# A two-layer hybrid block on one core: normed activations in one tile per chunk, and a pad ahead of the gated tiles

## The chip, the cores and the metric

The kernel runs on one core of one Trainium2 chip. The metric is device time in microseconds (us); the median of three runs of the kernel before is 1625.59 us (1624.21 to 1625.91).

## The reference

Two layers (DEPTH = 2) work on 256 latent tokens and 256 context tokens of width 1024, in float32. Each layer is a half-step SwiGLU FFN, a mixing stage of four head groups (Fourier, latent attention, spatial gating, pooling) between one input and one output projection, and a second half-step FFN. Norms are modulated by vectors computed from a conditioning vector with a 1024 x 9216 matrix per layer.

```python
def ffn_half_step(h, g, shift, scale, gate, w13, w2):
    return h + 0.5 * gate * swiglu(modulate(rms_norm(h, g), shift, scale), w13, w2)
...
def swiglu(x, w13, w2):
    a, b = jnp.split(x @ w13, 2, axis=-1)
    return (jax.nn.silu(a) * b) @ w2
```

with D_FF = 2816. In the last layer the context tokens are not carried past the keys and values, so the last FFN works on the 256 latent tokens alone.

## The kernel before, in words

**Layout.** Activations are feature-major: 8 chunks (KC) of 128 features on the partitions, tokens along the columns, T = 256 latent columns ("half" v = 0) and 256 context columns (v = 1). The residual stream h stays in SBUF. Weights come from HBM as half-units of 128 x 1024 float32 (512 KB), each loaded by the SP queue into one of five staging tiles (`stg`).

**Two parts per number.** Every large product is made of three float32r matmuls (`mm3`, lines 191 to 193). ScalarE copies a staged half-unit rounded to float32r into `whi` (line 157), VectorE, or now and then GpSimd, subtracts to get the remainder `wlo` (line 165). In the same way an activation x becomes `xhi` + `xlo`. Line 191 multiplies whi by xhi, line 192 whi by xlo, line 193 wlo by xhi; all three add into one PSUM tile. The weights are the stationary operand (a 128 x 128 block of a half-unit, loaded anew for every matmul), the activations the moving one (512 columns for both halves of the tokens, 256 for one).

**The tiles of the activations.** The norm's output, and in the mixing stage the four groups' outputs, stand in `nhi0..7` and `nlo0..7`, one pair per chunk, each [128, 2T + 2] (lines 516 and 517). `n_of(c, v)` gives the slices of half v, or both halves. The gated products silu(a) b stand in `ghi0..7` and `glo0..7`, [128, 512] each, allocated in each FFN's own pool. Of the FFN's 22 k-blocks, three parts of 8, 7 and 7 are worked off in turn: the part's first products (w13 against n, "n" below), then its second products (w2 against g, "g" below). In the third part the last four output tiles are done half by half, 256 columns at a time (`final_half`).

**The last FFN's raw form.** Before the last FFN the norm's factors are not waited for: its first products take A h, with the shift as extra columns (`raw_of`, `raw_shifts`, `raw_in`), so these matmuls have 258 columns; the factor 1/rms, kept in a tile `rsb`, is multiplied in behind them. There `raw_of(c)` uses the v = 1 half and the two extra columns of nhi and nlo.

**Addresses.** SBUF tiles are placed pool after pool in the order in which the program opens them, each rounded up to 32 bytes. Per partition, in bytes: the `whi` tiles start at 76480 and the `wlo` tiles at 96960, five of 4096 bytes each; a block of weights begins at a multiple of 512 from there. So every block of weights lies at 192 modulo 256, which is called the weights' residue here. `nhi0` starts at 117440 and the sixteen nhi and nlo tiles follow with a stride of 2080 (2056 rounded up), so that their residues modulo 256 are 192, 224, 0, 32, 64, 96, 128, 160 for chunks 0 to 7, the same for nhi and nlo (nlo0 starts 16640 = 65 x 256 bytes behind nhi0). The pool `tmp` follows, and after it, from 165248 on, the pools of a stage. In the first FFN a pool `early` of 9280 bytes and a table of 8192 come before the gated tiles: they start at 182720 with strides of 2048, residue 192. In the second, third and last FFN the pool starts at 165248 and all its tiles have residue 128.

**Order of work.** The order of all instructions on each engine is fixed when the program is built. `Weaver` keeps an estimate of TensorE's time (`W.pe`) and resumes the side tasks (norms, evacuations, weight conversion, the modulation's dot products on VectorE) when their estimated turn has come; the estimated costs depend on the operands' shapes, not on their addresses.

Of the kernel before, what the change touches and what calls it, by code (L numbers as in the profile page):

```python
# [11 lines left out]
F32 = mybir.dt.float32  # L12
# [19 lines left out]

# columns of the per-layer parameter packs
PK1 = {}
# [19 lines left out]
class Weaver:  # L54
    """Keeps an estimate of TensorE's time and resumes side tasks when their turn comes."""

# [48 lines left out]
class Slots:  # L105
    """A fixed set of equal tiles, handed out in the order in which they came back."""

# [21 lines left out]
def block_kernel(ctx: ExitStack, tc: tile.TileContext, ins, out: bass.AP):  # L129
# [10 lines left out]

    # ---------------------------------------------------------------- pools
    cst = ctx.enter_context(tc.tile_pool(name="cst", bufs=1))
# [11 lines left out]

    # ---------------------------------------------------------------- engine helpers
    def act(o, i, func, after=0.0, n=None, **kw):
# [42 lines left out]

    # ---------------------------------------------------------------- the weight stream  # L200
    loads = []
# [121 lines left out]

    # ---------------------------------------------------------------- constants and residual
    ident = cst.tile([P, P], F32, name="ident")
# [40 lines left out]

    # ---------------------------------------------------------------- modulation
    mods, gains, gates, n_ada, n_mod = {}, {}, {}, {}, {}
# [14 lines left out]
    def gain_from(l, i, c0=0, c1=KC, n=2):  # L383
        """A = sqrt(D) g (1 + scale) for norm i."""
        m = mods[l][:, :n, (1, 4, 7)[i] * 8 + c0:(1, 4, 7)[i] * 8 + c1]
        vstt(gains[l][:, i, :n, c0:c1], m, 1.0,
             gains[l, "g"][:, i, None, c0:c1].to_broadcast([P, n, c1 - c0]), ALU.add, ALU.mult)
# [16 lines left out]
    def ada_quarter(q, tiles):  # L404
        """Layer 0's m0 and m1, column chunks 2q and 2q+1."""
        ps = yield from SM.get()
        for k, (when, w) in enumerate(tiles):
            yield when
            for g in range(4):
                nc.tensor.matmul(ps[32 * g:32 * g + 32, :P], sc[:, k], w[:, 128 * g:128 * g + 128],  # L410
                                 start=k == 0, stop=k == KC - 1)
            W.pe(270.0)
        yield W.t + 150.0
        sb = yield from DG.get()
        yield vcopy(sb[:, :P], ps[:, :P])
        tp = ps[:, P:]
        yield transpose(tp[:, :P], sb[:, :P])
        DG.put(sb)
        b = k1(0, "b_ada")
        for v in range(2):  # L420
            for m in range(2):
                o = 8 * m + 2 * q
                src = tp[:, :P].rearrange("p (g r) -> p g r", r=32)[:, 2 * m:2 * m + 2, v]
                vtt(mods[0][:, v, o:o + 2], src, b[:, o:o + 2], ALU.add)
        SM.put(ps)
        gain_from(0, 0, 2 * q, 2 * q + 2)
        n_ada[0] += 4
        yield W.free["v"]

    def ada_tile(j, l, i):  # L430
        """128 columns of the modulation: VectorE's dot products of w_ada's columns with silu(c)."""
        r, c = i // KC, i % KC
# [20 lines left out]

    # ---------------------------------------------------------------- norms
    last = [False]
    acc, acc_i, acc_n, acc_t, last_sq = {}, {}, {}, {}, {}

    def square_in(v, c):
        """Adds the squares of h's chunk c, half v, to half v's sum."""
        if v not in acc:  # L460
# [19 lines left out]
    def sum_of(v):  # L480
        """Waits for half v's sum of squares; gives it with the time it is there."""
        while acc_n.get(v, 0) < KC:
# [5 lines left out]
    def rstd_chain(srcs, nblk, n_feat):  # L488
        """1/sqrt(sum + n eps) of the columns of src [128, 128 nblk], broadcast over partitions (in PSUM)."""
        ps = yield from SM.get()  # L490
# [24 lines left out]
    n_time = {}  # L515
    nhi = [npl.tile([P, 2 * T + 2], F32R, name="nhi%d" % c) for c in range(KC)]
    nlo = [npl.tile([P, 2 * T + 2], F32R, name="nlo%d" % c) for c in range(KC)]

    def n_of(c, v):
        s = slice(0, 2 * T) if v is None else slice(v * T, v * T + T)  # L520
        return nhi[c][:, s], nlo[c][:, s]

    # The last norm's factors are applied behind the first products: these take A h with the shift as one more column.
    raw_done = set()
    raw_R = []

    def raw_of(c):
        return nhi[c][:, T:], nlo[c][:, T:]

    def raw_shifts(l, i):  # L530
        for c in range(KC):
            s = shift_of(l, i, 0, c).to_broadcast([P, 2])
            hi, lo = (t[:, 2 * T:] for t in (nhi[c], nlo[c]))
            yield act(hi, s, AF.Copy)
            yield vtt(lo, s, hi.bitcast(F32), ALU.subtract)

    def raw_in(l, i, c):
        hi, lo = n_of(c, 1)
        x, a = h[:, c, 0], gain_of(l, i, 0, c)
# [3 lines left out]

    def apply(l, i, v, R, c0=0, c1=KC):
        """The modulated norm of h's chunks c0..c1, half v, as an exact sum of two float32r parts."""
        prev = None
# [16 lines left out]
    def norm_task(l, i, v):  # L563
# [4 lines left out]
        if raw_done:  # L568
            R = tmp.tile([P, T], F32, name="rsb", tag="rsb", bufs=1)
            yield act(R, ps[:, :T], AF.Copy)  # L570
# [4 lines left out]

    # ---------------------------------------------------------------- GEMM pieces
    hi_ = [0]
# [9 lines left out]
    def cols(ps, vs):  # L587
        """The columns of a PSUM tile that hold the halves vs."""
        return ps[:, vs[0] * T:(vs[-1] + 1) * T]

    def gemm(i, vs, nk=KC, xs=None, ps=None, ok=None, raw=False):
        """A feature-major tile: half-unit i against all k, halves vs."""
        ps = ps or ps_new()
# [10 lines left out]
    def gemm_start(i0, vss, evacs, ks=range(KC), ok=None, raw=False):  # L604
        """The four half-units at i0, half by half, k outermost, behind what makes their operand."""
        ok = ok or (lambda v, k: n_done.get(v, 0) > k)
# [22 lines left out]

    # ---------------------------------------------------------------- FFN  # L630
    def ffn(l, which, vs, tail):
        """h += 0.5 m (silu(a) b) w2 with a, b from the norm's output. Ends with the squares of the new h."""
        i_norm = (0, 2)[which - 1]
        full = len(vs) == 2
        with tc.tile_pool(name="ffn%d%d" % (l, which), bufs=2) as fp:
            ghi = [None] * 8
            glo = [None] * 8
# [111 lines left out]
    def final_half(vs, nk, xs, upd, tail, ok, raw=None):  # L749
        """The last eight M-tiles: the second four half by half, with h's squares and the norms behind them."""  # L750
        if xs:
# [29 lines left out]
    def fill():  # L781
        """Starts the modulation's tiles whose turn has come."""
        while ada_next[0] < len(ada_at):
# [15 lines left out]

    # ---------------------------------------------------------------- start  # L800
    def start_units(i0, evacs, fp, ST, GT):
        """The modulation's first columns, the first norm and the first half-units, in the order of arrival."""
        n_units = HI
# [47 lines left out]
        def chain(v):  # L851
            """The norm's factors of half v."""
            t = []
# [77 lines left out]

    # ---------------------------------------------------------------- mixing
    def mixing(l, tail):
# [4 lines left out]
        with ExitStack() as es:  # L938
# [23 lines left out]

            # -- blockdiag(C_c w_f), blockdiag(-S_c w_f)
            def bd_task():
# [13 lines left out]

            # -- q, k, v
            tb = Slots(W, mp, "tb", [P, 512], F32, TB)  # L980
# [106 lines left out]

            # -- attention
            def scores(v, hd, qb, pt):
                """exp of the scores, normalised and transposed into pt, for one block of queries."""  # L1090
                k0 = 0 if v == 0 else T
# [32 lines left out]
            def attention(v):  # L1124
                """All heads of half v's queries."""
                k0 = 0 if v == 0 else T
# [37 lines left out]

            # -- gating
            def y_of(g, j, v):
# [43 lines left out]

            # -- Fourier
            def fourier(v):
# [37 lines left out]

            # -- pooling
            def pooling(v):
# [30 lines left out]

            # -- the stream of projections
            gemm_start(i0, [vs, vs, [0, 1], [0, 1]], [ev_q, ev_kv])
# [57 lines left out]

    # ---------------------------------------------------------------- the two layers
    def norm_next(l, i):
# [34 lines left out]

# [1 line left out]
def _tiles(w):  # L1382
    """[K, M] -> [M/128, 128 (k in chunk), K/128, 128 (m)]"""
    k, m = w.shape
# [38 lines left out]
def _half_swap(w):  # L1423
    """Swaps the two halves of each rope axis in the last 32 columns' axis."""
    s = w.shape[:-1]
# [88 lines left out]
```

## Time and profile before

| what | before |
|---|---|
| median of three runs | 1625.59 us (1624.21 to 1625.91) |
| profiled execution: span from first to last instruction | 1622.2 us |
| TensorE busy with matmuls | 1583.4 us (98%), 8862 matmuls |
| TensorE loading weights, beside matmuls | 1339.3 us (83%) |
| VectorE, ScalarE, GpSimd busy | 1020.5, 556.9, 145.2 us |
| mean DMA rate | 151 GB/s |

The stages, in us from the span's start: start and first FFN 0 to 401, mixing of layer 0 to 598, second FFN to 938, third FFN (layer 1's first) 975 to 1314, mixing of layer 1 to 1433, last FFN to 1612, last norm to 1622. [...]

### The profile page before, as it was taken

The numbers are of one execution on the slowest core, as the hardware profiler recorded it, in microseconds if no ns is written. First come the engines' busy times: TensorE is split into PE (matmuls) and PEld (weight loads), VectorE is DVE, ScalarE is ACT, GpSimd is POOL, SyncE is SP. The second block draws the span as 40 slices with busy tenths as digits, with TensorE's granted clock in tenths as the row PEclk, the third lists the DMA queues.
The fourth block names the chain that finished last, engine by engine and source line by source line (L and its number), as shares of the span: only waits on it lengthen the run. The fifth ranks groups of instructions, "written<-read, shape, count | busy, mean of one in ns | idle before, by whom it ended". The sixth has DMA issues, their size and how long they took to land.

```text
span 1622.2 us, 22411 instructions
## 1 busy us (share of the span) xinstructions
PE 1583.4 (98%) x8862; PEld 1339.3 (83%) x8862; DVE 1020.5 (63%) x1693; ACT 556.9 (34%) x845; POOL 145.2 (9%) x115
## 2 busy tenths in 40 slices
PE   5999999999999999999999999999999999999997
PEld 3788888888867998888888898888888887899997
DVE  4568777877757476465563366776464367776674
ACT  3332221233534352222222243222222245554443
POOL 2000000004211320000000130000000051220001
PEclk9999999999999999999999999999999999999999
DMA  9355655654211144343352225566463222255452
GB/s 355 144 188 195 195 191 172 225 181 166 88 44 53 54 180 156 127 156 136 124 168 95 87 74 178 177 209 232 169 222 136 84 103 93 88 191 183 166 200 72
DMA packets 72057, 245.53 MB, mean 151 GB/s; under 512 B 8336, under 2 KB 10640, under 8 KB 71184
## 3 DMA queue, kind: packets, MB, share of 16 engines
q1 hardware_dynamic: 71664, 243.71, 44.0%
q8 instruction: 69, 1.13, 0.3%
q10 hardware_dynamic: 288, 0.39, 0.1%
q14 instruction: 36, 0.29, 0.1%
HBM read 243.03 MB, written 1.05 MB: 150 GB/s over the span
## 4 chain that ended last, share of the span: by engine, by line
PE 93%; DVE 5%; ACT 1%; issue 1%; DMA 0%; POOL 0%; SPq 0%; DVEq 0%; ACTq 0%; POOLq 0%
PE mm L191 28%; PE mm L193 28%; PE mm L192 28%; PE mm L184 5%; DVE nlo L169 2%; PE mm L197 1%; PE mm L1325 1%; PE mm L410 1%; DVE nt L169 1%; PE mm L1326 1%; PE mm L1327 1%; DVE wlo L165 0%; PE mm L1309 0%; PE mm L1310 0%; PE mm L1311 0%
## 5 line engine op out<-in xcount | busy, mean ns | idle before, releaser
L191 PE MATMUL mm<-nhi,whi 128*128 128x512 f32 (+2 forms) x1802 | 627.9, 348 | 3.1 <-ACT whi L157 3.1
L192 PE MATMUL mm<-nlo,whi 128*128 128x512 f32 (+2 forms) x1802 | 621.0, 345 | 10.1 <-DVE nlo L169 10.0
L193 PE MATMUL mm<-nhi,wlo 128*128 128x512 f32 (+2 forms) x1802 | 622.1, 345 | 1.0 <-DVE wlo L165 0.9
L157 ACT ACTIVATE whi<-stg 128x1024 fp32r<-128x1024 f32 (+1 forms) x310 | 318.1, 1032 | 434.8 <-PE mm L192 171.5
L165 DVE TENSOR_TENSOR wlo<-stg,whi 128x1024 fp32r<-128x1024 f32 (+1 forms) x288 | 347.7, 1211 | 89.2 <-ACT whi L157 88.7
L192 PEld LDWEIGHTS mm<-nlo,whi 128*128 128x128 f32 x1802 | 341.1, 189 | 58.7 <-DVE nlo L169 12.5
L191 PEld LDWEIGHTS mm<-nhi,whi 128*128 128x128 f32 x1802 | 340.6, 189 | 51.3 <-issue 4.4
L193 PEld LDWEIGHTS mm<-nhi,wlo 128*128 128x128 f32 x1802 | 340.5, 189 | 46.7 <-DVE wlo L165 1.7
L436 DVE SCALAR_TENSOR_TENSOR junk<-stg,sbc 128x1024 bf16<-128x1024 f32 x224 | 274.6, 1226 | 8.1 <-DMA stg<-in_w_ada 6.1
L191 PE MATMUL mm<-ghi,whi 128*128 128x512 f32 (+1 forms) x788 | 271.7, 345 | 0.0
L192 PE MATMUL mm<-glo,whi 128*128 128x512 f32 (+1 forms) x788 | 271.1, 344 | 0.0
L193 PE MATMUL mm<-ghi,wlo 128*128 128x512 f32 (+1 forms) x788 | 270.9, 344 | 0.0
L474 POOL TENSOR_TENSOR acc<-acc,sq 128x256 f32<-128x256 f32 x68 | 66.1, 978 | 1291.6 <-ACT sq L157 1123.7
L169 DVE SCALAR_TENSOR_TENSOR h<-mm,gates,h 128x256 f32<-128x256 f32 x168 | 75.6, 480 | 150.2 <-PE mm L193 150.2
L192 PEld LDWEIGHTS mm<-glo,whi 128*128 128x128 f32 x788 | 148.5, 188 | 19.6
L191 PEld LDWEIGHTS mm<-ghi,whi 128*128 128x128 f32 x788 | 148.6, 189 | 19.3
L193 PEld LDWEIGHTS mm<-ghi,wlo 128*128 128x128 f32 x788 | 148.3, 188 | 19.2
L165 DVE TENSOR_TENSOR g<-mm,s 128x512 f32<-128x512 f32 x66 | 45.6, 690 | 180.6 <-PE mm L193 179.9
L157 ACT ACTIVATE ghi<-g 128x512 fp32r<-128x512 f32 (+1 forms) x88 | 50.9, 579 | 286.7 <-DVE g L165 274.3
L157 ACT ACTIVATE nhi<-nt,mods 128x256 fp32r<-128x256 f32 x80 | 39.0, 506 | 84.1 <-DVE nt L169 84.0
L165 DVE TENSOR_TENSOR glo<-g,ghi 128x512 fp32r<-128x512 f32 (+1 forms) x88 | 54.5, 620 | 18.2 <-ACT ghi L157 18.2
L303 POOL TENSOR_TENSOR wlo<-stg,whi 128x1024 fp32r<-128x1024 f32 x22 | 55.7, 2535 | 61.7 <-ACT whi L157 61.2
(151 smaller groups left out, 854.3 us busy)
## 6 DMA issues: line engine op xcount, KB each, us to landing
stg<-in_w_ffn SPq DMA_DIRECT2D x208, 512.0 KB, 4.2
stg<-in_w_ada SPq DMA_DIRECT2D x128, 512.0 KB, 3.6
stg<-in_w_ffn SPq DMA_DIRECT2D x64, 448.0 KB, 3.1
stg<-in_w_in SPq DMA_DIRECT2D x22, 512.0 KB, 3.3
stg<-in_w_out SPq DMA_DIRECT2D x16, 512.0 KB, 3.4
sbc<-in_cb SPq DMA_DIRECT2D x3, 1024.0 KB, 7.0
pk<-in_pk SPq DMA_DIRECT2D x2, 1344.0 KB, 7.4
h<-in_xT SPq DMA_DIRECT2D x4, 512.0 KB, 6.0
```

The lines of the kernel that those rows point to most:

```text
L157: nc.scalar.activation(o, i, func, **kw)
L165: nc.vector.tensor_tensor(out=o, in0=a, in1=b, op=op)
L169: nc.vector.scalar_tensor_tensor(out=o, in0=a, scalar=s, in1=b, op0=op0, op1=op1)
L184: nc.tensor.matmul(o, l, r, start=first, stop=last, skip_group_check=skip)
L191: nc.tensor.matmul(o, wh, xh, start=first, stop=False, skip_group_check=skip)
L192: nc.tensor.matmul(o, wh, xl, start=False, stop=False, skip_group_check=skip)
L193: nc.tensor.matmul(o, wl, xh, start=False, stop=last, skip_group_check=skip)
L197: nc.tensor.transpose(o, i, ident)
L303: nc.gpsimd.tensor_tensor(out=lo[:, :n], in0=raw, in1=hi[:, :n].bitcast(F32), op=ALU.subtract)
L410: nc.tensor.matmul(ps[32 * g:32 * g + 32, :P], sc[:, k], w[:, 128 * g:128 * g + 128], start=k == 0, stop=k == KC - 1)
L436: nc.vector.scalar_tensor_tensor(out=ada_tiles["junk"], in0=stage[j], scalar=1.0, in1=ada_tiles["s"][:, v], op0=ALU.mult, op1=ALU.mult, ac ...
L474: nc.gpsimd.tensor_tensor(out=acc[v], in0=acc[v], in1=s, op=ALU.add)
```

## The change

The eight pairs nhi, nlo become eight tiles `n0..7` of [128, 4T + 64] = 1088 columns (4352 bytes = 17 x 256), in the order hi of v = 0, lo of v = 0, hi of v = 1, lo of v = 1, and 64 columns of which the raw form uses four. With both halves asked for, `n_of` now gives two runs of 256 columns that lie 512 columns apart, instead of 512 columns in a row. `raw_of` takes hi from column 512 on (258 columns) and lo behind it, from column 770.

In every FFN but the first, a tile `pad` of 16 columns (64 bytes) is allocated ahead of the pool's other tiles, and set to zero on VectorE. The copy of the last norm's factor goes to one of the three `nt` tiles instead of a tile `rsb` of its own.

```diff
-    nhi = [npl.tile([P, 2 * T + 2], F32R, name="nhi%d" % c) for c in range(KC)]
-    nlo = [npl.tile([P, 2 * T + 2], F32R, name="nlo%d" % c) for c in range(KC)]
+    nt_ = [npl.tile([P, 4 * T + 64], F32R, name="n%d" % c) for c in range(KC)]
 
     def n_of(c, v):
-        s = slice(0, 2 * T) if v is None else slice(v * T, v * T + T)
-        return nhi[c][:, s], nlo[c][:, s]
+        if v is None:
+            a = nt_[c][:, :4 * T].rearrange("p (v x) -> p v x", v=2)
+            return a[:, :, :T], a[:, :, T:]
+        o = 2 * T * v
+        return nt_[c][:, o:o + T], nt_[c][:, o + T:o + 2 * T]
...
     def raw_of(c):
-        return nhi[c][:, T:], nlo[c][:, T:]
+        o = 2 * T
+        return nt_[c][:, o:o + T + 2], nt_[c][:, o + T + 2:o + 2 * T + 4]
...
-            hi, lo = (t[:, 2 * T:] for t in (nhi[c], nlo[c]))
+            hi, lo = (t[:, T:] for t in raw_of(c))
...
     def raw_in(l, i, c):
-        hi, lo = n_of(c, 1)
+        hi, lo = (t[:, :T] for t in raw_of(c))
...
-            R = tmp.tile([P, T], F32, name="rsb", tag="rsb", bufs=1)
+            R = yield from NT.get()
...
         with tc.tile_pool(name="ffn%d%d" % (l, which), bufs=2) as fp:
+            if (l, which) != (0, 1):
+                nc.vector.memset(fp.tile([P, 16], F32, name="pad", tag="pad", bufs=1), 0.0)
```

The rest of the diff takes out comments and docstrings.

## Rows read from the trace of the kernel before

**Rows 1.** Page, part 1: busy us, share of the span and instructions of each engine.
```profile
PE 1583.4 (98%) x8862; PEld 1339.3 (83%) x8862; DVE 1020.5 (63%) x1693; ACT 556.9 (34%) x845; POOL 145.2 (9%) x115
```

**Rows 2.** Page, part 4: the chain that ended last, its shares by engine.
```profile
PE 93%; DVE 5%; ACT 1%; issue 1%; DMA 0%; POOL 0%; SPq 0%; DVEq 0%; ACTq 0%; POOLq 0%
```

**Rows 3.** Waits of TensorE, whole span: us in total, times, longest us.
```profile
PE mm L192 <- DVE nlo L169: 10.0, 11, 1.6
```

**Rows 4.** Groups by shape, TensorE, whole span: operands, count | busy us, mean ns | idle.
```profile
L191 PE MATMUL mm<-nhi,whi 128*128 128x512 f32 x990 | 392.4, 396 | 0.0
...
L191 PE MATMUL mm<-ghi,whi 128*128 128x512 f32 x444 | 174.7, 393 | 0.0
...
L191 PE MATMUL mm<-nhi,whi 128*128 128x256 f32 x460 | 135.8, 295 | 3.1 <-ACT whi L157 3.1
...
L191 PE MATMUL mm<-nhi,whi 128*128 128x258 f32 x352 | 99.7, 283 | 0.0
...
L191 PE MATMUL mm<-ghi,whi 128*128 128x256 f32 x344 | 97.0, 282 | 0.0
```

**Rows 5.** The same view, 131 to 174 us: first FFN, second products.
```profile
L191 PE MATMUL mm<-ghi,whi 128*128 128x512 f32 x64 | 24.9, 389 | 0.0
```

**Rows 6.** The same view, 668 to 708 us: second FFN, second products.
```profile
L191 PE MATMUL mm<-ghi,whi 128*128 128x512 f32 x57 | 22.5, 396 | 0.0
```

**Rows 7.** The same view, 176 to 251 us: first FFN, first products.
```profile
L191 PE MATMUL mm<-nhi,whi 128*128 128x512 f32 x108 | 42.7, 396 | 0.0
```

**Rows 8.** The same view, 714 to 787 us: second FFN, first products.
```profile
L191 PE MATMUL mm<-nhi,whi 128*128 128x512 f32 x106 | 41.9, 396 | 0.0
```

**Rows 9.** Timeline of TensorE: start us, length us, instruction; 134 to 174 us.
```profile
133.62 0.39 PE L191 MATMUL mm<-ghi,whi 128*128 128x512 f32 x1
...
173.96 0.39 PE L192 MATMUL mm<-glo,whi 128*128 128x512 f32 x1
```

**Rows 10.** Timeline of TensorE, 668 to 708 us.
```profile
667.73 0.40 PE L192 MATMUL mm<-glo,whi 128*128 128x512 f32 x1
...
707.87 0.40 PE L193 MATMUL mm<-ghi,wlo 128*128 128x512 f32 x1
```

**Rows 11.** Timeline of TensorE, 712 to 752 us.
```profile
711.83 0.39 PE L192 MATMUL mm<-nlo,whi 128*128 128x512 f32 x1
...
751.82 0.40 PE L193 MATMUL mm<-nhi,wlo 128*128 128x512 f32 x1
```

**Rows 12.** Timeline of TensorE, 390 to 399 us: first FFN, one half of tokens.
```profile
389.73 0.28 PE L192 MATMUL mm<-glo,whi 128*128 128x256 f32 x1
...
398.97 0.28 PE L191 MATMUL mm<-ghi,whi 128*128 128x256 f32 x1
```

**Rows 13.** Timeline of TensorE, 928 to 937.5 us: second FFN, one half.
```profile
927.82 0.28 PE L192 MATMUL mm<-glo,whi 128*128 128x256 f32 x1
...
937.48 0.28 PE L193 MATMUL mm<-ghi,wlo 128*128 128x256 f32 x1
```

**Rows 14.** Timeline of TensorE, 1534.5 to 1551.5 us: last FFN, second part.
```profile
1534.26 0.28 PE L192 MATMUL mm<-glo,whi 128*128 128x256 f32 x1
...
1551.43 0.28 PE L192 MATMUL mm<-glo,whi 128*128 128x256 f32 x1
```

**Rows 15.** Timeline of TensorE, 535 to 555 us: mixing, one half.
```profile
534.82 0.28 PE L191 MATMUL mm<-nhi,whi 128*128 128x256 f32 x1
...
554.91 0.28 PE L193 MATMUL mm<-nhi,wlo 128*128 128x256 f32 x1
```

**Rows 16.** Timeline of TensorE, 1555 to 1577 us: last FFN, 258 columns.
```profile
1554.73 0.29 PE L193 MATMUL mm<-nhi,wlo 128*128 128x258 f32 x1
...
1576.89 0.28 PE L192 MATMUL mm<-nlo,whi 128*128 128x258 f32 x1
```

**Rows 17.** Busy time of each engine in one stretch, 131 to 388 us.
```profile
131.00:388.00 257.00, 257.00 (x1119) 209.55 (x1118) 203.76 (x313) 69.86 (x85) 6.07 (x4) 1.00 0.58 191
```

**Rows 18.** Groups of VectorE, 186 to 263 us: a small instruction.
```profile
L169 DVE SCALAR_TENSOR_TENSOR gains<-mods,g 128x16 f32<-128x16 f32 x1 | 0.2, 176 | 0.0
```

## The prediction

> **What bounds the kernel now.** I read the page's busy times first: TensorE has matmuls in flight for 1583.4 us of the span [rows 1]. The chain of waits confirms it: 93% of what ended last is TensorE's own work [rows 2]. The waits come third: the largest one of TensorE in the loop stages, for the norm's lower part from VectorE, is 10.0 us over the whole span [rows 3]. So the time is the sum of the distances between matmul starts, and the question is what sets one distance.
>
> The groups by shape give the counts. Each row of line 191 has two sisters (lines 192 and 193) with the same count, so there are 3 x 990 = 2970 matmuls of 512 columns on n, 3 x 444 = 1332 on g, 1380 and 1056 on n with 256 and 258 columns, and 1032 on g with 256 [rows 4].
>
> Now compare the same matmul in two stages. On g, with 512 columns, one lasts 389 ns in the first FFN and 396 ns in the second [rows 5, 6]. It isn't the stage: on n, one lasts 396 ns in both FFNs [rows 7, 8]. What differs between the two g cases is where the g tiles lie: residue 192 modulo 256, the weights' own, in the first FFN, and 128 in the others. The n tiles have eight residues, the same in all stages.
>
> Distances between starts say it without the modelled ends. First FFN, g: 178 distances from 133.62 to 173.96 us, 226.6 ns each [rows 9]. Second FFN, g: 172 distances from 667.73 to 707.87, 233.4 ns [rows 10]. n, 512 columns: 172 distances from 711.83 to 751.82, 232.5 ns [rows 11]. With 256 columns the sign turns: 77 distances of 120.0 ns in the first FFN with g on the weights' residue [rows 12], 82 of 117.8 ns in the second without [rows 13], and only 150 of 114.5 ns in the last FFN's second part [rows 14].
>
> **The change, part by part.** The new n tiles have a stride of 4352 = 17 x 256 bytes from the unchanged base 117440, so each starts at residue 192; lo lies 1024 bytes behind hi and v = 1 another 1024 on, so every part that `n_of` gives is on the weights' residue. The n tiles take 34816 bytes instead of 33280 (+1536), and `rsb` goes (-1024), so the stage pools begin 512 bytes later: same residues. The 64-byte pad then moves the g tiles of the last three FFNs from 128 to 192.
>
> 1. n with 512 columns: I take the distance of the first FFN's g, 226.6 ns, for 232.5. 2970 x 5.9 ns = -17.5 us. Upper bound for one distance: two runs of 256 columns as two matmuls of 120.0 = 240.0 ns, since no row shows a moving operand in two runs. Lower bound: 226.6, the least distance of 512 columns in any row. I take it because both runs keep the residue and the number of columns.
> 2. g with 512 columns in the second and third FFN: the first FFN has a third of the 1332 (three like FFNs), so 888 x (233.4 - 226.6 = 6.8) = -6.0 us. This is the same operand, shape and order as in rows 9, at the same residue: the surest term.
> 3. g with 256 columns. Per FFN the four last tiles are 4 x 7 blocks x 3 matmuls x 2 halves = 168; the second and third FFN pay 336 x (120.0 - 117.8) = +0.7 us. The last FFN has 22 x 8 x 3 = 528: the first part's 192 at the second FFN's distance +0.4, the other 336 at 120.0 - 114.5 = +1.8. Together +3.0 us; the other end is no loss, 0.
> 4. n with 256 columns: 170 distances of 118.2 ns in the mixing stage [rows 15]; at 120.0, 1380 x 1.8 = +2.5 us at most, since some stand behind waits. Other end: 114.5, which is -5.1.
> 5. The raw form, 258 columns: 185 distances of 119.8 ns [rows 16]. hi comes to residue 192, but lo lies 1032 bytes behind it, at 200, which nothing before has. From the aligned 120.0 and two columns more (226.6 - 120.0 for 256 columns, 0.4 ns each) 120.8; 1056 x 1.0 = +1.1 us. Ends: 114.5 (-5.6) and, with lo as far above its neighbours as g was on the wrong side with 512 columns, 6.8 ns on all: +7.2.
> 6. The mixing stage's products with n as the stationary operand (144 of 512 columns and 144 of 256, counted from the loops) change by the same distances, -0.8 and +0.3: -0.5 us.
> 7. The pads: three memsets of 16 columns on VectorE. The nearest row is 176 ns for 16 columns [rows 18]; queued behind each are the norm's products that TensorE waits for at a stage's start [rows 3], so at most 3 x 0.18 = 0.5 us; I take 0, as the memset is issued while TensorE still has its last output tiles. The memory under a pad belonged to q or to a tile s of the stage before, whose last readers are done some output tiles earlier, so I expect no wait there. The factor's copy into an `nt` tile is the same ScalarE instruction; the three nt tiles have no other user in the last FFN.
> 8. Order and dependences: the estimates depend on shapes, and two runs of 256 make the same 512, so every queue keeps its order; no DMA moves. A read of both halves' hi now spans the first half's lo as well, but every such read outside the start comes after both were written. What else might get late is VectorE: 203.8 of 257 us busy in the first FFN's densest stretch [rows 17]; cut by 2.6% to 250 us, it would be 81% busy. That cover holds.
>
> [...]
>
> Sum: -17.5 - 6.0 + 3.0 + 2.5 + 1.1 - 0.5 = -17.4 us. The profiled span is 1622.2 us, 3.4 us less than the median of the runs, which I take as what lies around the span and unchanged. Span 1604.8, time 1625.6 - 17.4 = 1608.2 us.
>
> **The rivals.**
>
> A, half effect. The n tiles alternate between 192 and 448 modulo 512, the weights are at 192, and rows 9 show only a g tile 256 away from the weights modulo 512. If a finer address counts, or the stream settles in another rhythm, half of term 1 goes: +8.7, 1617 us. For it: with 256 columns at one residue (128) the trace has both 117.8 and 114.5 ns [rows 13, 14], so one residue has more than one rhythm. Against: with 512 columns the rows hold one value over whole parts.
>
> B, the change doesn't do what it says. If the first FFN's g is faster for some other reason than its address, terms 1 and 2 vanish and so do 3 to 6: 1625.6 us. For it: only one stage has aligned tiles. Against: n is the same in both FFNs [rows 7, 8].
>
> C, slower. The mechanism is the moving operand in two runs: if the array's feed restarts at the jump as it does at a matmul's start, a 512-column product costs two of 256, 240.0 ns, in all 2970 places. Term 1 becomes 2970 x 7.5 = +22.3, the sum +22.4: 1648 us. It decides from 5.9 ns a jump, where terms 1 to 6 come to nothing, and from 7.0 ns (1.1 ns x 2970 = 3.3 us more) the kernel is slower by what can be measured. No row has such an operand, so none excludes it; that I give it little is judgement: the 240.0 ns would need a whole second start inside one instruction.
>
> D, the losses don't come. 256 and 258 columns stay as they are, terms 3 to 5 vanish: 1601.6 us. The two rhythms above speak for it, the steady 120.0 ns of rows 12 against it.
>
> **How the numbers follow.** Forecast 0.66, A 0.12, B 0.05, C 0.05, D 0.12. What a measurement of this kernel can tell from no change is about 0.2%, 3.3 us. Forecast, A and D are faster: 0.90; same 0.05; slower 0.05. The range runs from 1601, just under D, to A's 1617; it takes in the raw form's +6.1 on the forecast (1614), and leaves out B and C.
>
> **What would show each step.** In the profile after: starts in the n stretches of 512 columns 226 to 227 ns apart, all chunks alike, and the group's mean near 389 ns instead of 396 (term 1; 232 says B, near 240 says C, chunks taking turns says A); g in the second and third FFN at 389 instead of 396 (term 2); g of one half at 120 in all FFNs, the last one included (term 3, else D); the 258-column group's mean by line, with line 192, which reads lo, apart from the others (term 5). TensorE's waits for VectorE should stay near 10 us (terms 7, 8). The prediction is wrong if n and g with 512 columns don't get the same distance, or if the time leaves 1601 to 1617.

## The result, and the profile after

Changed kernel: 1608.93 us median of four runs (1606.6 to 1609.86), against 1625.75 us for the kernel before in the same job. The ratio is 0.9897, 95% interval 0.9883 to 0.991: faster by 1.0%. The profiled execution has a span of 1604.8 us, before 1622.2.

The page after shows the same picture as [rows 1, 2] with less matmul time: 1566.2 us of TensorE instead of 1583.4, and the chain still TensorE's own.

```profile
PE 1566.2 (98%) x8862; PEld 1345.5 (84%) x8862; DVE 1020.8 (64%) x1696; ACT 557.2 (35%) x845; POOL 145.3 (9%) x115
...
PE 93%; DVE 4%; ACT 1%; issue 1%; DMA 0%; POOL 0%; SPq 0%; DVEq 0%; ACTq 0%; POOLq 0%
```

The groups of TensorE by shape (operands, count | busy us, mean ns | idle) answer to [rows 4].

```profile
L191 PE MATMUL mm<-n,whi 128*128 128x512 f32 x990 | 386.0, 390 | 0.0
L192 PE MATMUL mm<-n,whi 128*128 128x512 f32 x990 | 385.2, 389 | 0.0
L193 PE MATMUL mm<-n,wlo 128*128 128x512 f32 x990 | 385.1, 389 | 0.0
L191 PE MATMUL mm<-ghi,whi 128*128 128x512 f32 x444 | 172.7, 389 | 0.0
...
L192 PE MATMUL mm<-n,whi 128*128 128x258 f32 x352 | 100.9, 287 | 2.0 <-DVE n L169 2.0
L191 PE MATMUL mm<-n,whi 128*128 128x258 f32 x352 | 100.2, 285 | 0.0
L193 PE MATMUL mm<-n,wlo 128*128 128x258 f32 x352 | 99.9, 284 | 0.3 <-DVE wlo L165 0.3
L191 PE MATMUL mm<-ghi,whi 128*128 128x256 f32 x344 | 98.1, 285 | 0.0
```

All products of 512 columns now last 389 to 390 ns, the value that only the first FFN's g had in [rows 5]. In the 258-column group line 192 (it reads lo) stands apart: 287 ns, where lines 191 and 193 have 285 and 284.

The timeline gives the distances between starts. A matmul of 512 columns on n is listed with 0.39 us and followed by the next one's start 0.23 us later (703.66, then 703.89 us in the profile after); the time it takes from the stream is read here as that distance. Below are first and last rows of stretches without a break: n with 512 columns (177 distances), g in the second FFN (172), n with 256 in the mixing stage (168), n with 258 (166), g of the last FFN's second part (109).

```profile
703.66 0.39 PE L192 MATMUL mm<-n,whi 128*128 128x512 f32 x1
...
743.78 0.39 PE L192 MATMUL mm<-n,whi 128*128 128x512 f32 x1
...
660.82 0.39 PE L192 MATMUL mm<-glo,whi 128*128 128x512 f32 x1
...
699.81 0.39 PE L193 MATMUL mm<-ghi,wlo 128*128 128x512 f32 x1
...
529.83 0.28 PE L193 MATMUL mm<-n,wlo 128*128 128x256 f32 x1
...
549.99 0.28 PE L193 MATMUL mm<-n,wlo 128*128 128x256 f32 x1
...
1473.72 0.28 PE L193 MATMUL mm<-n,wlo 128*128 128x258 f32 x1
...
1493.88 0.28 PE L191 MATMUL mm<-n,whi 128*128 128x258 f32 x1
...
1517.82 0.28 PE L193 MATMUL mm<-ghi,wlo 128*128 128x256 f32 x1
...
1530.90 0.28 PE L191 MATMUL mm<-ghi,whi 128*128 128x256 f32 x1
```

Divided out: 226.7, 226.7, 120.0, 121.4 and 120.0 ns, where [rows 11, 10, 15, 16, 14] gave 232.5, 233.4, 118.2, 119.8 and 114.5. The long ones got shorter, the short ones longer, as forecast.

The 114.5 of [rows 14] needs a closer look, since that stretch is not without a break. Timeline of the kernel before, the start of that part:

```profile
1533.09 0.28 PE L191 MATMUL mm<-ghi,whi 128*128 128x256 f32 x1
...
1535.33 0.39 PE L192 MATMUL mm<-glo,whi 128*128 128x256 f32 x1
1535.55 0.28 PE L193 MATMUL mm<-ghi,wlo 128*128 128x256 f32 x1
```

Up to the break, one distance of 0.22 us, the starts are 117.7 ns apart; from 1536.02 us to the last row of [rows 14] they are 113.3 ns apart. So the same products, with every tile at the same place modulo 256, held two steady values one after the other, and 114.5 is a mean over both and the break. The mean over the whole part, breaks included, is 114.6 ns before and 120.4 after.

### The profile page after: what moved, and what is told of

The parts are those of the page before. It is cut to its first block, busy times and chain, and to the rows that moved or that the text cites. A ratio compares the mean times of both kernels' runs of the same rounds, so it can differ in the third digit from the quotient of the medians.

```text
span 1604.8 us, 22414 instructions
## 1 busy us (share of the span) xinstructions
PE 1566.2 (98%) x8862; PEld 1345.5 (84%) x8862; DVE 1020.8 (64%) x1696; ACT 557.2 (35%) x845; POOL 145.3 (9%) x115
## 4 chain that ended last, share of the span: by engine, by line
PE 93%; DVE 4%; ACT 1%; issue 1%; DMA 0%; POOL 0%; SPq 0%; DVEq 0%; ACTq 0%; POOLq 0%
PE mm L191 28%; PE mm L192 28%; PE mm L193 28%; PE mm L184 5%; DVE n L169 2%; PE mm L197 1%; PE mm L1331 1%; PE mm L410 1%; PE mm L1333 1%; PE mm L1332 1%; DVE nt L169 0%; DVE wlo L165 0%; PE mm L1315 0%; PE mm L1316 0%; DMA h<-in_xT 0%
## 5 line engine op out<-in xcount | busy, mean ns | idle before, releaser
L192 PE MATMUL mm<-n,whi 128*128 128x512 f32 (+2 forms) x1802 | 619.5, 344 | 9.8 <-DVE n L169 9.4
L191 PE MATMUL mm<-n,whi 128*128 128x512 f32 (+2 forms) x1802 | 622.9, 346 | 3.1 <-ACT whi L157 3.0
L193 PE MATMUL mm<-n,wlo 128*128 128x512 f32 (+2 forms) x1802 | 616.8, 342 | 0.9 <-DVE wlo L165 0.8
L157 ACT ACTIVATE whi<-stg 128x1024 fp32r<-128x1024 f32 (+1 forms) x310 | 318.1, 1032 | 430.9 <-PE mm L192 178.0
L192 PEld LDWEIGHTS mm<-n,whi 128*128 128x128 f32 x1802 | 342.2, 190 | 52.0 <-DVE n L169 12.2
L191 PEld LDWEIGHTS mm<-n,whi 128*128 128x128 f32 x1802 | 342.2, 190 | 46.7 <-issue 4.2
L193 PEld LDWEIGHTS mm<-n,wlo 128*128 128x128 f32 x1802 | 342.6, 190 | 40.2 <-DVE wlo L165 1.6
L191 PEld LDWEIGHTS mm<-ghi,whi 128*128 128x128 f32 x788 | 149.3, 189 | 17.4
L193 PEld LDWEIGHTS mm<-ghi,wlo 128*128 128x128 f32 x788 | 149.3, 189 | 17.3
L157 ACT ACTIVATE n<-nt,mods 128x256 fp32r<-128x256 f32 x80 | 38.9, 505 | 83.5 <-DVE nt L169 83.4
```

Source lines behind the costliest of these rows:

```text
L157: nc.scalar.activation(o, i, func, **kw)
L191: nc.tensor.matmul(o, wh, xh, start=first, stop=False, skip_group_check=skip)
L192: nc.tensor.matmul(o, wh, xl, start=False, stop=False, skip_group_check=skip)
L193: nc.tensor.matmul(o, wl, xh, start=False, stop=last, skip_group_check=skip)
```

## The experiments

Theory R: the distance between matmuls depends on where the moving operand lies against the weights, modulo 256 bytes, and for 512 columns equality is best. Each run is read by its own stretches first, since a time mixes all terms. Where a span alone is given, the kernel ran once.

**a1_spread: the old residues in the new layout.** One tile per chunk and two runs per operand stay; each chunk's slices move by 32 bytes times its number.

```diff
+    def off(c):
+        return 8 * c
...
-            a = nt_[c][:, :4 * T].rearrange("p (v x) -> p v x", v=2)
+            a = nt_[c][:, off(c):off(c) + 4 * T].rearrange("p (v x) -> p v x", v=2)
...
-        o = 2 * T * v
+        o = off(c) + 2 * T * v
...
-        o = 2 * T
+        o = off(c) + 2 * T
```

> The changed kernel, with the slices in each n tile moved by 8 columns (32 bytes) per chunk, so that the eight chunks again have the eight residues of the kernel before, still one tile per chunk and two runs per operand. Theory R (the residue against the weights' sets the distance): the 512-column products on n go back from 226.7 to about 232.5 ns, 2970 x 5.8 = +17 us, span about 1620; g with 512 columns stays at 226.7. Rival L (one tile with hi beside lo, or two runs, is what helps): all distances stay, span about 1605.

Span 1620.1 us. Timeline, n with 512 columns, 173 distances:

```profile
710.71 0.39 PE L193 MATMUL mm<-n,wlo 128*128 128x512 f32 x1
...
750.93 0.39 PE L192 MATMUL mm<-n,whi 128*128 128x512 f32 x1
```

232.5 ns, the old value to a tenth, while g of the second FFN kept 226.9. Summed over all 2970 of these matmuls, the distances come to 691.7 us, against 691.8 in the kernel before and 674.7 in the changed one. So for these products the layout (hi beside lo, two runs of 256) neither gains nor costs anything; the residues are the whole of it. This also settles rival C of the prediction.

**a2_n128: one residue for all chunks, but not the weights'.**

```diff
+    def off(c):
+        return 32
```

with `off(c)` used as in a1_spread.

> The changed kernel, with the slices in every n tile moved by 32 columns (128 bytes): all chunks share one residue, 64 modulo 256, but the weights stay at 192. Theory R (equal to the weights' residue is what counts): 512 columns on n at about 233 ns, +19 us, span about 1624, with 256 columns at 114 to 118 instead of 120. Rival U (it's enough that all activations share one residue, so that the stream keeps one rhythm): 512 columns stay at 226.7, span about 1605. If the pattern repeats every 128 bytes, as U.

Span 1623.6 us. n with 512 columns, 172 distances:

```profile
711.82 0.39 PE L191 MATMUL mm<-n,whi 128*128 128x512 f32 x1
...
751.96 0.39 PE L192 MATMUL mm<-n,whi 128*128 128x512 f32 x1
```

233.4 ns: a common residue alone is worth nothing, and rival U falls. The 256-column products on n went to 118.7 ns.

**a3_pad_only: the kernel before with the three pads.**

```diff
+            if (l, which) != (0, 1):
+                nc.vector.memset(fp.tile([P, 16], F32, name="pad", tag="pad", bufs=1), 0.0)
```

> The kernel before, with nothing but the three pads. Theory R with terms that add: g with 512 columns 233.3 to 226.7 in the second and third FFN, -6.0 us, g with 256 columns +3.0, so -3.0 us: about 1622.7. n with 512 columns stays at 232.5. Rival K (what a product on n leaves behind decides the rhythm on g): g stays near 233 in both, time about 1625.7.

Time 1621.01 us, ratio 0.9971 (0.9962 to 0.9981) to the kernel before. g of the second FFN, then n, 172 distances each:

```profile
668.82 0.39 PE L193 MATMUL mm<-ghi,wlo 128*128 128x512 f32 x1
...
707.80 0.39 PE L191 MATMUL mm<-ghi,whi 128*128 128x512 f32 x1
...
712.83 0.40 PE L192 MATMUL mm<-nlo,whi 128*128 128x512 f32 x1
...
752.81 0.40 PE L193 MATMUL mm<-nhi,wlo 128*128 128x512 f32 x1
```

226.6 and 232.4 ns: the two parts of the change act on their own products only, and their gains add; rival K falls. The median fell 4.6 us below the kernel before's 1625.6 in the same job, 1.6 us further than expected, while the two profiled spans differ by 2.3 us (1619.9 against 1622.2). The distances explain 3 us; the rest is not placed, and the ten runs spread over 5.8 us.

**a5_all64: weights, n and g all 64 bytes up.**

```diff
+    shp = ctx.enter_context(tc.tile_pool(name="shp", bufs=1))
+    nc.vector.memset(shp.tile([P, 16], F32, name="shift64"), 0.0)
     hip = ctx.enter_context(tc.tile_pool(name="hip", bufs=HI))
```

> The changed kernel, with a 64-byte tile in front of the weights' tiles, so that weights, n and g all move up by 64 bytes: all residues are 0 modulo 256, their differences unchanged. Theory R (only the difference to the weights counts): every distance as in the changed kernel, span about 1605. Rival S (residue 192 itself is a good place): 512 columns on n and g go to 229 to 237 ns, span 1616 to 1640.

Span 1607.9 us; n with 512 columns, 177 distances:

```profile
708.83 0.39 PE L195 MATMUL mm<-n,wlo 128*128 128x512 f32 x1
...
748.95 0.39 PE L195 MATMUL mm<-n,wlo 128*128 128x512 f32 x1
```

226.7 ns: only the difference counts, not the place. The span is 3.1 us longer with the same distances: 2.8 us of it arise at the two places of the mixing stage that are shown under c2.

**b1_n64, b2_n16, b3_n192: other distances from the weights.** `off(c)` returns 16, 4 and 48 columns, and the pads of the second, third and last FFN are 24, 48, 0; 8, 40, 24; and 80, 32, 48 columns.

> The changed kernel with n 64 bytes past the weights' residue, g 32 bytes past it in the second FFN (pad of 24 columns), 128 past it in the third (48), 64 short of it in the last (no pad). Theory R with equality as the only good place: n with 512 columns at 229 to 237 ns, g with 512 columns likewise in both; span 1618 to 1632. Rival P (the pattern repeats every 64 or 32 bytes, or some other distance is as good): one of these stretches at 226.7 or below. Last FFN's g: 114 to 118 ns instead of 120.

> The changed kernel with n 16 bytes past the weights' residue, g 32 bytes short of it in the second FFN (pad of 8 columns), 96 past it in the third (40), 32 past it in the last (24). Theory R with equality as the only good place: n with 512 columns between 227 and 235 ns (16 bytes off is close, so it may be little), g with 512 columns 229 to 237; span 1608 to 1632. Rival P: a stretch at 226.7 or below at one of these distances.

> The changed kernel with n 192 bytes past the weights' residue (64 short of the next), g 256 bytes past it in the second FFN (pad of 80 columns), 64 past it in the third (32), 128 past it in the last (48). Theory R with a period of 256 bytes: g in the second FFN stays at 226.7 ns although it is now 256 bytes off; n with 512 columns at about 233 ns as g was before at the same 64 bytes short; g in the third FFN 229 to 237; span 1618 to 1630. Rival Q (a period of 512 bytes or more): g in the second FFN leaves 226.7.

Spans 1612.0, 1629.0 and 1620.1 us. For b1 the forecast missed: its span lies under 1618 to 1632, because n at +64 bytes came out at 228.9 ns, a little under the 229 to 237 that equality as the only good place asked for. b2 and b3 lie in their ranges. Timeline of b1_n64, n with 512 columns at +64 bytes, 176 distances:

```profile
709.62 0.39 PE L191 MATMUL mm<-n,whi 128*128 128x512 f32 x1
...
749.90 0.39 PE L193 MATMUL mm<-n,wlo 128*128 128x512 f32 x1
```

Timeline of b2_n16, n at +16 bytes, 174 distances:

```profile
714.62 0.39 PE L193 MATMUL mm<-n,wlo 128*128 128x512 f32 x1
...
754.92 0.40 PE L193 MATMUL mm<-n,wlo 128*128 128x512 f32 x1
```

Timeline of b3_n192: g of the second FFN at +256 bytes (178 distances), g of the third at +64 (176), and with 256 columns there (90).

```profile
668.64 0.39 PE L192 MATMUL mm<-glo,whi 128*128 128x512 f32 x1
...
708.98 0.39 PE L193 MATMUL mm<-ghi,wlo 128*128 128x512 f32 x1
...
1040.68 0.39 PE L192 MATMUL mm<-glo,whi 128*128 128x512 f32 x1
...
1080.96 0.39 PE L191 MATMUL mm<-ghi,whi 128*128 128x512 f32 x1
...
1298.73 0.28 PE L193 MATMUL mm<-ghi,wlo 128*128 128x256 f32 x1
...
1308.93 0.28 PE L193 MATMUL mm<-ghi,wlo 128*128 128x256 f32 x1
```

With the stretches of all these runs read in this way, the distance between starts by the bytes between operand and weights, modulo 256:

| bytes past the weights' residue | ns, 512 columns | ns, 256 columns |
|---|---|---|
| 0, and 256 (b3) | 226.7 | 120.0 |
| 16 (n in b2) | 231.6 | 117 to 119 |
| 32 (g in b1, b2) | 233.3 | 117 to 118 |
| 64 (n in b1, g in b3 and c1) | 228.9 | 113.3 to 117.8 |
| 96 (g in b2) | 233.4 | 120 |
| 128 (n in a2, g in b1, b3) | 232.3 to 233.4 | 118.6 to 120 |
| 192 (n in b3, g before and in b1, b4) | 233.3 | 113.3 to 117.8 |
| 224 (g in b2) | 233.3 | 118 |

With 512 columns equality is the best of those tried, 64 bytes the next; 16 bytes off costs most of the gain (4.9 of 6.7 ns). The same bytes give the same value on n and on g, to 1 ns at 128. A period of 128 bytes is ruled out by a2; 256 fits, since +256 behaves as 0. Rival P found nothing at or below 226.7 with 512 columns, rival Q falls.

**b4_nopad12: no pad in the last FFN.**

```diff
-            if (l, which) != (0, 1):
+            if (l, which) in ((0, 2), (1, 1)):
```

> The changed kernel without the pad in the last FFN, whose g products have 256 columns alone. Theory R with a loss at 256 columns when on the residue: 528 products go from 120 to the 117.8 and 114 ns of the kernel before, -2.4 us: about 1606.3 against 1608.9, the best so far. Rival: the rhythm that the aligned n leaves behind holds g at 118 to 120 whatever its place: -0 to -1 us.

1605.67 us (1603.47 to 1608.38), ratio 0.9884 (0.9867 to 0.99) to before. g of the last FFN, first part (154 distances), second (150):

```profile
1449.76 0.28 PE L192 MATMUL mm<-glo,whi 128*128 128x256 f32 x1
...
1467.89 0.28 PE L193 MATMUL mm<-ghi,wlo 128*128 128x256 f32 x1
...
1512.81 0.28 PE L192 MATMUL mm<-glo,whi 128*128 128x256 f32 x1
...
1529.99 0.28 PE L192 MATMUL mm<-glo,whi 128*128 128x256 f32 x1
```

117.7 and 114.5 ns, as before the change (the second stretch again holds a break of 0.22 us, and 113.3 ns behind it). Summed over the 1032 products of g with 256 columns, the distances are 2.3 us less than in the changed kernel, against 2.4 expected: the pad in the last FFN cost that much. The ratios alone could not show it, as their intervals overlap (0.9867 to 0.99 here, 0.9883 to 0.991 with the pad).

**c1_best and c2_after_again.** c1 takes what the table offers: pad of 32 columns (+64 bytes) in the last FFN, and `raw_of` 16 columns (64 bytes) further on. c2 is the changed kernel itself on the same chip.

```diff
+            n_pad = {(0, 2): 16, (1, 1): 16, (1, 2): 32}.get((l, which), 0)
...
     def raw_of(c):
-        o = 2 * T
+        o = 2 * T + 16
```

> The changed kernel with each width where the runs so far had it lowest: the last FFN's g, 256 columns alone, 64 bytes past the weights' residue (pad of 32 columns), and the raw form's two parts 64 bytes further (258 columns); all 512-column operands stay on the residue. Theory R with the map of distances: g of the last FFN 120 to 113.3 ns, 528 x 6.6 = -3.5 us; 258 columns 121.4 to 120.0, 1056 x 1.4 = -1.5 us; about 1604 and a span near 1600. Rival (the map belongs to the stage in which it was read): g of the last FFN at 117 to 118 and 258 columns unchanged, -1.2 us, about 1607.7.

> The changed kernel as it is, beside c1 on the same chip. About 1608.9 and a span near 1604.8; every distance as in its first profile, since nothing in it depends on the chip or the run.

c1: 1603.73 us (1601.82 to 1606.67), ratio 0.9862 (0.9846 to 0.9879). c2: 1608.97 us (1606.4 to 1610.42), ratio 0.9897 (0.9882 to 0.9912). c1, 258 columns (168 distances) and g of the last FFN's second part (120):

```profile
1474.72 0.28 PE L192 MATMUL mm<-n,whi 128*128 128x258 f32 x1
...
1494.88 0.28 PE L192 MATMUL mm<-n,whi 128*128 128x258 f32 x1
...
1516.79 0.28 PE L191 MATMUL mm<-ghi,whi 128*128 128x256 f32 x1
...
1530.92 0.28 PE L191 MATMUL mm<-ghi,whi 128*128 128x256 f32 x1
```

258 columns: 120.0 ns instead of 121.4, as hoped. g: 117.8 and not the 113.3 that the same 64 bytes gave in b3's third FFN. So with 256 columns one distance in bytes has more than one steady value, and my table does not say which will come. The forecast's -3.5 us for g became 528 x 2.2 ns = -1.2 us, as its rival had it. The distances account for 528 x 2.2 + 1056 x 1.4 = 2.6 of the 5.2 us between the medians of c1 and c2. The rest of that is not placed, as most of these runs have no trace. c1 is not told apart from b4 (their intervals overlap).

c2 also shows where a difference of about 4 us between two executions of one kernel can lie. Its span is 1608.6 us against 1604.8 in the changed kernel's first profile, with the same 226.7 and 120.0 ns in the FFNs. Matched matmul by matmul, 0.9 us arises before 54 us, 1.3 us between 409 and 416 and 1.5 us between 572 and 585. The windows 410 to 440 and 560 to 600 us of the first profile and of c2's (the third column from the right is TensorE's granted clock):

```profile
410.00:440.00 30.00, 30.00 (x229) 28.89 (x229) 18.67 (x35) 17.09 (x30) 2.24 (x3) 1.00 0.24 78
560.00:600.00 40.00, 38.45 (x291) 36.99 (x290) 29.48 (x48) 22.21 (x34) 11.96 (x8) 1.00 0.49 168
```

```profile
410.00:440.00 30.00, 29.31 (x210) 28.30 (x210) 18.23 (x33) 17.09 (x30) 1.93 (x3) 0.94 0.17 54
560.00:600.00 40.00, 38.45 (x293) 37.61 (x293) 28.62 (x49) 19.21 (x32) 13.00 (x9) 0.96 0.41 150
```

The granted clock is 1.00 in the one and 0.94 and 0.96 in the other. At the first of the two places, before the first row's products, both profiles have the same wait for the norm's lower part (in brackets); the last two rows are c2's starts behind it:

```profile
409.76 0.38 PE L192 MATMUL mm<-n,whi 128*128 128x256 f32 x1 [1.53 <-DVE n L169]
```

```profile
410.69 0.39 PE L192 MATMUL mm<-n,whi 128*128 128x256 f32 x1 [1.53 <-DVE n L169]
...
412.22 0.41 PE L191 MATMUL mm<-n,whi 128*128 128x256 f32 x1
412.43 0.41 PE L192 MATMUL mm<-n,whi 128*128 128x256 f32 x1
```

c2's starts are 0.21 us apart there, and 0.12 in the first profile. After the same wait of 1.53 us the granted clock from 410 to 440 us was 1.00 in one execution and 0.94 in the other, so the code alone does not decide it. It differs at other places too: c1's profile has 0.98 from 1320 to 1430 us, where the changed kernel and c2 have 1.00. In the stretches read above no two starts lie more than 0.24 us apart with 512 columns, or 0.13 with 256 and 258, save at the breaks named, which is why they tell more here than medians do.

## Why the prediction was right

The forecast was 1608.2 us and a span of 1604.8; measured 1608.93 and 1604.8. The mechanism held: the distances moved where and by what the terms said. That the span agrees to a tenth is luck, since the terms miss by up to 1.1 us each and the misses cancel. For the median, the 3.4 us added to the span were two things: 1.8 us that lie around the span in every run with both on record, and 1.6 us by which the profiled execution was faster than the median. The profiled execution after was 2.3 us faster than its median, so the step from span to median came to 4.1 us.

Both profiles hold the same 8862 matmuls in the same order, so the distance behind each can be compared with its partner's. By terms, from the steady distances and from these sums:

1. n with 512 columns: 2970 x (232.5 - 226.7) = -17.2 us; summed -17.1; forecast -17.5. The choice of the aligned g as its stand-in held, and the doubt on two runs per operand came to nothing (a1).
2. g with 512 columns: 888 x (233.4 - 226.7) = -5.9 us; summed -6.0, as forecast; a3 shows it alone.
3. g with 256 columns: summed +3.1 us (122.0 before, 125.1 after); forecast +3.0. The forecast read the 114.5 ns of [rows 14] as one rhythm; it is a mean over 117.7, a break and 113.3, which serves for the sum. Without the pad the last FFN's part of it is gone (b4).
4. n with 256 columns: 120.0 against 118.2 ns would be 1380 x 1.8 = +2.5 at most; summed +1.4, since some stand behind waits, as the term itself allowed. Taking the most it could be was the largest miss.
5. The raw form: 1056 x (121.4 - 119.8) = +1.7 us; summed +1.5; forecast +1.1. Line 192, whose lo lies 8 bytes off the residue, went from 282 to 287 ns, line 191 from 283 to 285, line 193 stayed at 284; the forecast had left lo's price between wide ends.
6. n as the stationary operand: forecast -0.5. The sum of distances of these 288 matmuls fell by 0.2 us.
7. The pads: three memsets of 72 ns, and nobody waited for them. TensorE's waits for the norm's lower part are 9.4 us, against 10.0 in [rows 3].
8. VectorE in the window 131 to 388 us: 207.9 us busy, 81%, as forecast, and no new wait.

The summed terms come to -17.3 us, forecast -17.4; small changes elsewhere, among them a first matmul 0.3 us later, all but cancel.

Rival A (half effect by a finer address) fell with b3's +256 bytes and with all chunks alike. Rival B fell with a1, C with a1, D with the 120.0 and 121.4 ns of 256 and 258 columns. That addresses matter for these float32r products is seen where nothing else moves: in a1 and a2 the distance goes from 226.7 to 232.5 and 233.4 ns, and in a5, where weights and operands move together, it stays at 226.7.

What makes the distance longer off the residue is not shown; shown is that the difference to the weights' address counts (226.7 ns in a5, 233.4 in a2, 233.3 on n in b3). One guess, not tried by a run, is that the writes of ScalarE and VectorE into the weights' tiles, which share the weights' residue, cost the time. The kernel before speaks against it: of the 172 distances of [rows 10], 94 pass with no instruction of ScalarE, VectorE or GpSimd on `whi` or `wlo`, and their mean is 233.35 ns; the other 78 have 233.32. No run left the weights' loads out (8862 beside 8862 matmuls in the pages before and after), so whether they have a part in it stays open.

## What to carry to other kernels

Where a long stream of matmuls reloads its weights each time, look at the distance between starts by tile and not at the mean: if one shape takes two values in two stages, compare the tiles' addresses modulo 256 with the weights'. Here tiles a few bytes longer than a power of two came to lie at eight residues. A stride of a multiple of 256 bytes, with a start on the weights' own residue, gave 2.5% on n with 512 columns (232.5 to 226.7 ns); the stride alone gave nothing (233.4 ns in a2). Do it by shape: products of 256 columns lost 1.5 to 5% on the same residue (118.2 to 120.0 ns on n, 114.6 to 120.4 on g of the last FFN's second part), so the last FFN, whose g products have only 256 columns, is better without the pad, by 2.3 us.

## What the runs showed of the hardware

- The distance of 512-column float32r matmuls ranges from 226.7 to 233.4 ns with the operand's address alone, and depends on the difference to the weights' address (226.7 in a5, where both move by 64 bytes); +256 bytes gives the value of 0 (226.7 in b3), +128 does not (233.4 in a2).
- With 256 columns the steady value at one distance in bytes is not fixed: 113.3 and 117.8 ns at +64 (b3, c1), and at 192 in the kernel before 117.7 and then 113.3 within one part, with a single distance of 0.22 us between them. What picks it is open; such a break does not always change it (c1 has one and stays at 117.8).
- An operand in two runs of 1024 bytes has the same distance as one in a single run of 2048: 232.5 ns in a1 and in [rows 11], and 226.7 on n and on g in the changed kernel.
- After one and the same wait of 1.53 us the granted clock from 410 to 440 us was 1.00 in one execution and 0.94 in another (c2); there two starts with 256 columns lie 0.21 us apart instead of 0.12.
